# A pool mixer, SGU and PEER block: the last 32 gathers move from a stage of their own into the loop over the dense experts

## The chip, the cores and the metric

One NeuronCore of one Trainium2 chip runs the kernel. The metric is device time in microseconds, the median of several runs. Engines are named as in the profile: PE (TensorE matmuls), PEld (its weight loads), DVE (VectorE), ACT (ScalarE), POOL (GpSimd) and SP (SyncE, which only issues transfers here).

## The reference

1024 tokens of width 1024 pass a mixer (causal pooling over four windows beside a gated spatial unit) and then a PEER layer: 8 heads, each with two lists of 128 keys; the top 16 of each list are combined, the best 16 of the 256 pairs name 16 of 16384 experts, so a token uses 128 experts. An expert is one row of `peer_u` and one row of `peer_v`.

```python
q = (xb @ wq).reshape(T, PEER_HEADS, 2, D_HALF)
s = jnp.einsum('thpd,phkd->thpk', q, keys)
s_top, i_top = lax.top_k(s, PEER_TOPK)
...
idx = jnp.take_along_axis(cand_i, best_pos, axis=-1)
gate = jax.nn.softmax(best_s, axis=-1)
u = u_tab[idx]; v = v_tab[idx]
act = jax.nn.gelu(jnp.einsum('td,thkd->thk', xb, u))
return jnp.einsum('thk,thkd->td', (gate * act), v)
```

The layer's result is added to the residual and a last rmsnorm with `final_g` follows.

## The kernel before, in words

The 1024 tokens are eight blocks of 128. Two methods compute the PEER layer. Blocks 2 to 5 (512 tokens, "dense") run over all 16384 experts: `dense` (L604) goes through 128 groups `c` of 128 experts. For each it loads 512 KB of `uT` and 512 KB of `peer_v` (SP, three buffers `raw`), splits each into a high and a low part (ACT `uh`, `vh`, DVE `ul`, `vl`, L131 and L132), makes 24 matmuls into `mu` (`mm3`, L139 to L141), a GELU on ACT (L644), the product with the gates `gc` on DVE (L645) and a split into `wh`, `wl`. After every third `c` (`GROUP = 3`, L43) `down` makes 144 matmuls into `mm` and DVE adds them to `hD` (L623). 128 is not a multiple of 3, so the last two `c` have a `down` of their own. At the end four `finish` calls (L545: ACT square sum, a reciprocal root in twelve small DVE instructions, DVE scaling at L551, and a store by SP at L552) write blocks 2 to 5.

Blocks 0, 1, 6 and 7 ("sparse") fetch the chosen rows. `gather` (L475) is one indirect DMA issued by POOL that brings 128 rows of 4 KB into a buffer. A U part (`sparse_u`, L491) has 128 gathers of `peer_u`, one for each of a token's experts, and a DVE dot product after each (`junk`, L501). A V part (`sparse_v`, L513) has 128 gathers of `peer_v`, one for each token, taken four at a time (a quad): ACT writes the weights into `wz` (L520; two copies in turn), and PE adds the four tokens' sums into `po` (L531, 16 matmul records for a quad). When the 32 quads of a block are through, the residual is loaded, DVE adds `po` to it (L542) and `finish` follows. Only the four blocks' U and V parts gather: 1024 gathers in all.

`sparse(EARLY)` (L808) issues the first 320 of them ahead of the dense experts. `sparse(LATE)` (L814) is a generator with 704 steps, one gather each: the rest of U1, then V1 beside U6, V6 beside U7, and last V7 alone. The loop at L817 to L820 runs `dense`, and after each group `c` it advances the generator, so that `done * 128 <= (c + 1) * (704 - AFTER)`: 672 steps over 128 groups, 5.25 a group. The remaining `AFTER = 32` steps, all of V7, run in a stage of their own (L822 to L826) with a pool `gae` of 16 buffers `rowe`. That pool is opened on the right side after the pool `da` of `dense` has closed, so it lies where `da` lay, the tiles `hD` among it. Beside the dense experts the gathers use `rowv` (4 buffers) and `rowt` (7 buffers); V7 alone takes both in turn, quad by quad.

Nothing runs in the order in which it is written. The framework's scheduler orders the instructions of each engine by priority (program order) and by its own estimate of when each one could start, and each engine then runs its list in order. The matmuls of a quad carry a higher priority (L527), so they stand in PE's list where the scheduler thought their rows would have come.

Of the kernel before, what the change touches and what calls it, by code (L numbers as in the profile page):

```python
# [27 lines left out]
NK = 128  # L28
# [14 lines left out]
GROUP = 3  # L43
# [7 lines left out]

TURN = 6

ROWS, VROWS, EROWS = 7, 4, 16
QUAD = 4

EARLY = ({"U0": 128}, {"V0": 128, "U1": 64})
LATE = ({"U1": 64}, {"V1": 128, "U6": 128}, {"V6": 128, "U7": 128}, {"V7": 128})

AFTER = 32  # L60

RUNS = ((0, 1, 16), (1, 7, 8), (8, 8, 1))
NC = sum(na * nb for _, na, nb in RUNS)
# [3 lines left out]
def hybrid_block(ctx: ExitStack, tc: tile.TileContext, t: dict, out: bass.AP):  # L67
# [405 lines left out]
    homes = {"U": [(gat, "rowt", ROWS)], "V": [(gat, "rowt", ROWS)]}  # L473
# [189 lines left out]
    beside = []  # L663

    def sparse(phases):


        for phase in phases:
            n = max(phase.values())
            if beside:  # L670
                kinds = {name[0] for name in phase}
                homes["U"] = beside[:1] if len(kinds) > 1 else beside
                homes["V"] = beside[1:] if len(kinds) > 1 else beside
            for i in range(n):
                for name, m in phase.items():
                    unit = QUAD if name[0] == "V" else 1
                    for _ in range(((i + 1) * m // n // unit - i * m // n // unit) * unit):
                        if name not in parts:
                            parts[name] = [(sparse_u if name[0] == "U" else sparse_v)(int(name[1:])), 0]
                        part = parts[name]  # L680
                        next(part[0])
                        part[1] += 1
                        if part[1] == P:
                            for _ in part[0]:
                                pass
                        yield
# [93 lines left out]
    steps = 8 + P // TB  # L780
# [33 lines left out]
    gathered = sparse(LATE)  # L814
    steps = sum(sum(phase.values()) for phase in LATE)
    done = 0
    for c in dense(de, xdh, xdl):  # L817
        while done * NK < (c + 1) * (steps - AFTER):
            next(gathered, None)
            done += 1  # L820

    with tc.tile_pool(name="gae", bufs=EROWS, side="right", reuse_waits="tile") as gae:  # L822
        beside[:] = [(gae, "rowe", EROWS)]
        homes["U"] = homes["V"] = beside[:]
        for _ in gathered:
            pass  # L826
    gavs.close()
    des.close()

# [37 lines left out]
```

## Time and profile before

| | us |
|---|---|
| median of 3 runs (2700.18 to 2703.74) | 2702.26 |
| the profiled execution's own time | 2707.89 |
| its span | 2705.8 |
| POOL's last gather beside the dense experts starts | 2495.6 |
| the last matmul of the dense experts starts | 2635.6 |
| the first gather of the last stage starts | 2646.23 |

The span is the stretch of the trace, and the own time lies 2.09 us above it. The 40 slices of the profile's page are 67.6 us each; PE is busy in nine tenths or more of every slice from the seventeenth to the thirty-ninth, and three tenths of the last.

### The profile page before, as it was taken

The numbers are of one execution on the slowest core, as the hardware profiler recorded it, in microseconds if no ns is written. First come the engines' busy times: TensorE is split into PE (matmuls) and PEld (weight loads), VectorE is DVE, ScalarE is ACT, GpSimd is POOL, SyncE is SP. The second block draws the span as 40 slices with busy tenths as digits, with TensorE's granted clock in tenths as the row PEclk, the third lists the DMA queues.
The fourth block names the chain that finished last, engine by engine and source line by source line (L and its number), as shares of the span: only waits on it lengthen the run. The fifth ranks groups of instructions, "written<-read, shape, count | busy, mean of one in ns | idle before, by whom it ended". The sixth has DMA issues, their size and how long they took to land.

```text
span 2705.8 us, 34765 instructions
## 1 busy us (share of the span) xinstructions
PE 2438.1 (90%) x11968; PEld 1862.7 (69%) x11968; DVE 1896.4 (70%) x4643; ACT 774.3 (29%) x1424; POOL 1198.3 (44%) x1098
## 2 busy tenths in 40 slices
PE   7997899888866467999999999999999999999993
PEld 6886788767645144777777777777777777766770
DVE  2389979987797977986776767666676766433451
ACT  3220011245635252222222222322222222222220
POOL 0034753143443544655555555465455555344004
PEclk9998999999978689999999999999999999999996
DMA  7677998599988799999999999899999999889317
GB/s 250 210 245 230 384 344 284 168 313 315 333 286 296 255 307 348 361 356 324 365 354 342 341 339 364 328 361 375 327 342 359 349 348 331 324 329 359 119 39 287
DMA packets 345392, 831.49 MB, mean 307 GB/s; under 512 B 25216, under 2 KB 158848, under 8 KB 345216
## 3 DMA queue, kind: packets, MB, share of 16 engines
q0 software_dynamic: 147456, 536.94, 54.0%
q1 hardware_dynamic: 197760, 292.33, 31.4%
q8 instruction: 95, 1.56, 0.2%
q14 instruction: 81, 0.66, 0.1%
HBM read 785.13 MB, written 44.04 MB: 306 GB/s over the span
## 4 chain that ended last, share of the span: by engine, by line
PE 67%; DVE 15%; DMA 9%; issue 5%; ACT 2%; POOL 1%; SPq 0%; POOLq 0%; ACTq 0%; DVEq 0%
PE mm L176 8%; PE mm L139 8%; PE mm L140 8%; PE mu L141 8%; PE mm L141 8%; PE mu L139 8%; PE mu L140 8%; PE po L531 8%; DVE junk L501 3%; DMA G<-gs 2%; DMA rowt<-peer_v,idxT 2%; DVE rest L372 1%; PE mm L582 1%; DMA w<-w_out 1%; PE mu L582 1%
## 5 line engine op out<-in xcount | busy, mean ns | idle before, releaser
L480 POOL DMA_INDIRECT rowt<-peer_v,idxT x432 | 500.5, 1159 | 709.0 <-PE po L531 501.6
L480 POOL DMA_INDIRECT rowv<-peer_u,idx x288 | 353.6, 1228 | 176.4 <-DVE junk L501 105.7
L480 POOL DMA_INDIRECT rowt<-peer_u,idx x224 | 261.4, 1167 | 346.5 <-DVE top L370 166.4
L139 PE MATMUL mm<-vh,wh 128*128 128x512 f32 x1024 | 400.8, 395 | 14.4 <-ACT wh L131 8.4
L141 PE MATMUL mu<-xdh,ul 128*128 128x512 f32 x1024 | 403.0, 394 | 6.6 <-DVE ul L132 6.6
L139 PE MATMUL mu<-xdh,uh 128*128 128x512 f32 x1024 | 401.2, 393 | 6.2 <-ACT xdh L131 3.7
L140 PE MATMUL mu<-xdl,uh 128*128 128x512 f32 x1024 | 401.8, 392 | 1.2 <-DVE xdl L132 0.7
L140 PE MATMUL mm<-vl,wh 128*128 128x512 f32 x1024 | 401.0, 392 | 0.1
L501 DVE SCALAR_TENSOR_TENSOR junk<-rowv,h 128x1024 bf16<-128x1024 f32 x288 | 352.0, 1222 | 44.2 <-DMA rowv<-peer_u,idx 41.2
L141 PE MATMUL mm<-vh,wl 128*128 128x512 f32 x1024 | 376.9, 392 | 0.0
L623 DVE TENSOR_TENSOR hD<-hD,mm 128x512 f32<-128x512 f32 x344 | 225.8, 682 | 184.4 <-PE mm L141 183.5
L501 DVE SCALAR_TENSOR_TENSOR junk<-rowt,h 128x1024 bf16<-128x1024 f32 x224 | 271.9, 1214 | 19.6 <-DMA rowt<-peer_u,idx 18.2
L531 PE MATMUL po<-rowt,wz 128*32 128x512 f32 x1728 | 237.8, 650 | 38.0 <-DMA rowt<-peer_v,idxT 38.0
L139 PEld LDWEIGHTS mm<-vh,wh 128*128 128x128 f32 x1024 | 193.0, 189 | 75.1 <-issue 14.2
L141 PEld LDWEIGHTS mu<-xdh,ul 128*128 128x128 f32 x1024 | 192.6, 188 | 65.8 <-DVE ul L132 9.4
L139 PEld LDWEIGHTS mu<-xdh,uh 128*128 128x128 f32 x1024 | 192.1, 188 | 58.7 <-issue 9.2
L140 PEld LDWEIGHTS mu<-xdl,uh 128*128 128x128 f32 x1024 | 192.8, 188 | 53.8 <-issue 9.2
L141 PEld LDWEIGHTS mm<-vh,wl 128*128 128x128 f32 x1024 | 192.6, 189 | 50.1 <-issue 9.2
L140 PEld LDWEIGHTS mm<-vl,wh 128*128 128x128 f32 x1024 | 193.2, 189 | 42.4 <-issue 2.5
L644 ACT ACTIVATE a<-mu 128x512 f32<-128x512 f32 x128 | 76.0, 594 | 491.2 <-PE mu L141 490.0
L132 DVE SCALAR_TENSOR_TENSOR ul<-raw_u,uh 128x1024 fp32r<-128x1024 f32 x128 | 156.2, 1220 | 78.3 <-ACT uh L131 78.3
L131 ACT ACTIVATE vh<-raw_v 128x1024 fp32r<-128x1024 f32 x128 | 131.0, 1052 | 235.8 <-PE mm L141 216.9
(167 smaller groups left out, 3374.3 us busy)
## 6 DMA issues: line engine op xcount, KB each, us to landing
raw_u<-uT SPq DMA_DIRECT2D x128, 512.0 KB, 6.9
raw_v<-peer_v SPq DMA_DIRECT2D x128, 512.0 KB, 7.2
G<-gs SPq DMA_DIRECT2D x32, 1024.0 KB, 14.8
w<-wq SPq DMA_DIRECT2D x48, 512.0 KB, 6.6
w<-w_in SPq DMA_DIRECT2D x36, 512.0 KB, 4.8
w<-w_out SPq DMA_DIRECT2D x24, 512.0 KB, 6.6
h<-x SPq DMA_DIRECT2D x16, 512.0 KB, 7.7
rowt<-peer_v,idxT POOLq DMA_INDIRECT x432
```

Of the source, the lines that this page charges most:

```text
L131: nc.scalar.activation(hi, src, AF.Copy)
L132: nc.vector.scalar_tensor_tensor(lo, src, 1.0, f32(hi), op0=ALU.mult, op1=ALU.subtract)
L139: nc.tensor.matmul(dst, lh, rh, start=first and c == 0, stop=False)
L140: nc.tensor.matmul(dst, lh, rl, start=False, stop=False)
L141: nc.tensor.matmul(dst, ll, rh, start=False, stop=last and c == n - 1)
L176: mm = nc.tensor.matmul(dst[:, i, :], lhs, rhs, start=c == 0, stop=c == NDC - 1)
L480: ins = nc.gpsimd.indirect_dma_start(out=rowt, out_offset=None, in_=t[table], in_offset=bass.IndirectOffsetOnAxis(ap=ids, axis=0))
L501: nc.vector.scalar_tensor_tensor(junk, r, 1.0, h, op0=ALU.mult, op1=ALU.mult, accum_out=act[:, j:j + 1])
L531: mm = nc.tensor.matmul(po[g * 32:(g + 1) * 32, q * HALF:(q + 1) * HALF], z[:, g, 31 - j:63 - j], r[:, q * HALF:(q + 1) * HALF], start=j = ...
L582: mm = nc.tensor.matmul(p[:, i, :], oh[:, i, :], c, start=True, stop=True)
L623: nc.vector.tensor_add(hq, hq, p)
L644: nc.scalar.activation(a, p, AF.Gelu_apprx_tanh)
```

## The change

The stage at the end, its pool and the constants `AFTER` and `EROWS` go. All 704 steps of `sparse(LATE)` run in the loop over the dense experts, spread over the first 125 groups (`NK - GROUP`), so 5.632 a group. The last 32 gathers take `rowv` and `rowt` buffers like the other gathers of V7.

```diff
-ROWS, VROWS, EROWS = 7, 4, 16
+ROWS, VROWS = 7, 4
...
-
-AFTER = 32
...
     for c in dense(de, xdh, xdl):
-        while done * NK < (c + 1) * (steps - AFTER):
+        while done * (NK - GROUP) < min(c + 1, NK - GROUP) * steps:
             next(gathered, None)
             done += 1
-
-    with tc.tile_pool(name="gae", bufs=EROWS, side="right", reuse_waits="tile") as gae:
-        beside[:] = [(gae, "rowe", EROWS)]
-        homes["U"] = homes["V"] = beside[:]
-        for _ in gathered:
-            pass
     gavs.close()
     des.close()
```

## Rows read from the trace of the kernel before

**Rows 1.** Busy time by stretch: from:to, length, each engine's busy us (instructions), granted clock, DMA, GB/s
```profile
1200.00:2200.00 1000.00, 999.80 (x4789) 749.12 (x4791) 697.00 (x1007) 271.64 (x384) 546.11 (x457) 1.00 0.95 348
2300.00:2500.00 200.00, 200.00 (x1048) 141.08 (x1047) 84.66 (x115) 53.29 (x86) 89.06 (x87) 1.00 0.90 336
2500.00:2640.00 140.00, 135.72 (x613) 109.53 (x611) 68.89 (x115) 37.96 (x52) 0.00 (x0) 1.00 0.26 87
2640.00:2706.00 66.00, 23.38 (x128) 5.59 (x128) 8.69 (x35) 2.41 (x8) 29.96 (x32) 0.69 0.74 289
```

**Rows 2.** What PE waited for, 1200 to 2640 (all): us in total, times, longest
```profile
PE mm L139 <- ACT wh L131: 0.9, 1, 0.9
```

**Rows 3.** What POOL waited for, 2300 to 2706
```profile
POOL rowe L480 <- DMA out<-hD: 149.7, 1, 149.7
POOL rowv L480 <- PE po L531: 84.8, 13, 19.6
```

**Rows 4.** Timeline of the end: start us, us, engine, line, operation [idle before <- releaser]
```profile
2635.85 0.69 DVE L623 TENSOR_TENSOR hD<-hD,mm 128x512 f32<-128x512 f32 x1
...
2643.08 1.28 DVE L551 SCALAR_TENSOR_TENSOR hD<-hD,r,fgrow 128x1024 f32<-128x1024 f32 x1
2646.23 0.94 POOL L480 DMA_INDIRECT rowe<-peer_v,idxT  x1 [149.72 <-DMA out<-hD]
2647.47 0.94 POOL L480 DMA_INDIRECT rowe<-peer_v,idxT  x1 [0.30 <-issue]
...
2684.72 0.94 POOL L480 DMA_INDIRECT rowe<-peer_v,idxT  x1 [0.30 <-issue]
...
2692.78 3.40 PE L531 MATMUL po<-rowe,wz 128*32 128x512 f32 x16 [3.14 <-DMA rowe<-peer_v,idxT]
...
2696.28 1.22 DVE L542 TENSOR_TENSOR h<-h,po 128x1024 f32<-128x1024 f32 x1 [51.92 <-PE po L531]
...
2701.03 1.28 DVE L551 SCALAR_TENSOR_TENSOR h<-h,r,fgrow 128x1024 f32<-128x1024 f32 x1
```

**Rows 5.** PE's timeline around one pair of quads among dense matmuls
```profile
2488.11 0.39 PE L139 MATMUL mu<-xdh,uh 128*128 128x512 f32 x1
2488.43 1.94 PE L531 MATMUL po<-rowv,wz 128*32 128x512 f32 x16
2490.17 1.94 PE L531 MATMUL po<-rowt,wz 128*32 128x512 f32 x16
2492.04 0.50 PE L140 MATMUL mu<-xdl,uh 128*128 128x512 f32 x1
2492.38 0.40 PE L141 MATMUL mu<-xdh,ul 128*128 128x512 f32 x1
2492.62 0.40 PE L139 MATMUL mu<-xdh,uh 128*128 128x512 f32 x1
```

**Rows 6.** Gathers by buffer: ns min/median/max, first and last start; and rowv's quads on PE
```profile
L480 POOL DMA_INDIRECT rowe<-peer_v,idxT x32: 933/937/940, 2646.2 to 2684.7; - x32
L480 POOL DMA_INDIRECT rowv<-peer_v,idxT x48: 932/937/1984, 2296.5 to 2494.3; - x48
L531 PE MATMUL po<-rowv,wz x192: 592/592/618, 2319.9 to 2509.5; 128*32 128x512 f32 x192
```

**Rows 7.** The page's list of DMA queues: packets, MB, share of 16 engines
```profile
q0 software_dynamic: 147456, 536.94, 54.0%
```

**Rows 8.** Who waited in ACT and DVE, 1200 to 2500: us in total, times, longest
```profile
ACT wz L520 <- PE po L531: 183.4, 72, 9.9
DVE h L542 <- PE po L531: 7.2, 2, 6.3
```

**Rows 9.** Matmuls into mu, then into mm, 1200 to 2200: busy us (records)
```profile
1200.00:2200.00 1000.00, 463.60 (x1928) 1.00 0.95 348
1200.00:2200.00 1000.00, 464.29 (x1944) 1.00 0.95 348
```

**Rows 10.** Busy time early in the dense experts, and DVE's costliest groups there
```profile
1030.00:1180.00 150.00, 125.89 (x509) 98.16 (x509) 133.69 (x203) 40.01 (x51) 86.83 (x64) 0.95 0.96 353
...
L501 DVE SCALAR_TENSOR_TENSOR junk<-rowv,h 128x1024 bf16<-128x1024 f32 x33 | 40.2, 1219 | 0.3
L501 DVE DVE_READ_ACCUMULATOR junk<-rowv,h 128x1 f32 x32 | 2.6, 81 | 0.0
```

## The prediction

> **What bounds the kernel now.** I read the busy time by stretch first. From 1200 to 2200 us PE is busy 999.8 of 1000 us at a granted clock of 1.00 (2.4 GHz), while the DMA engines are at 0.95 and 348 GB/s [rows 1]. Both are nearly full, so the next question is which of them makes the other wait. The list of PE's waits answers it: from 1200 to 2640 PE waits once, for 0.9 us, and never for a row or a load [rows 2]. The dense experts are bound by PE's own list of matmuls.
>
> The end looks different. Between 2500 and 2640 POOL does nothing, the DMA engines fall to 0.26, and PE goes on; between 2640 and 2706 POOL and the DMA engines are back and PE has 23.4 of 66 us, at a mean granted clock of 0.69, so in part at 1.2 GHz [rows 1]. POOL's waits name the reason: one wait of 149.7 us, of the first gather into `rowe` for the store of `hD` [rows 3]. The pool `gae` lies where `hD` lay, so the last 32 gathers can't start before the dense result is on its way out, although POOL's last gather of the loop had started at 2495.6. The timeline of the end gives the order [rows 4]: the last scaling of `hD` ends at 2643.08 + 1.28 = 2644.36, the first late gather starts at 2646.23, the last quad at 2692.78, and block 7's own last scaling ends at 2702.31. The span ends at 2705.8. So some 61 us lie behind the dense result, and they are a chain of gathers, not matmul work.
>
> **The change part by part.** *What goes.* Everything between the end of the last scaling of `hD` (2644.36) and the same point of block 7 (2702.31), that is 57.95 us. Behind either there is one store, and 2705.8 - 2702.31 = 3.49 us until the span ends [rows 4]. I take 3.49 us behind `hD` too.
>
> *What is added to PE.* 32 gathers are 8 quads, 128 matmul records. PE is full, so they aren't hidden, and they push the dense end back. One pair of quads beside the dense experts shows the price [rows 5]: a dense matmul starts at 2488.11 and the next but for the pair at 2492.04, which is 3.93 us, where dense matmuls alone start 0.23 us apart (2492.38 to 2492.62 is 0.24, already nearly there). The pair costs 3.70 us plus 0.11 us for the slow step after it (2492.04 to 2492.38 is 0.34). A few hundredths more follow, so 3.9 us. Four pairs are 15.6 us. The bounds: 14.8 us (4 x 3.70) from below; from above, every quad alone with its own two switches, some 8 x (3.70/2 + 0.3) = 17.2 us. In the old stage the same quads ran at 0.69 of the clock and up to 3.40 us each [rows 4], which the change takes away without my counting it twice: it is in the 57.95.
>
> *What is added to POOL and the DMA engines.* V7's first 12 pairs have their `rowv` quads between 2319.9 and 2509.5 [rows 6], eleven steps of some 17 us. POOL waits 84.8 us in this part for PE to free a buffer [rows 3], so PE's list sets this pace, not the gathers. Four more pairs at 17 us put the last quad near 2511 + 4 x 17 = 2580, some 70 us ahead of a dense end near 2652. The bytes: 1024 gathers move 536.94 MB, 0.524 MB each [rows 7], so 32 are 16.8 MB. In 2500 to 2640 only 87 GB/s x 140 us = 12.2 MB move; with the gathers 29 MB in 156 us, 186 GB/s, where 336 and 348 run without a wait of PE [rows 1, 2]. I count POOL and transfers at nothing. Without that cover the price would be their own time at the old stage's rate, 16.8 MB / 289 GB/s = 58 us.
>
> The notes speak against such a cover. The Trainium skill, SBUF — State Buffer, section "SBUF: two separate sides", says that POOL writes the descriptors of its own DMAs and is locked out while certain VectorE operations run, so that such a gather stands still. The row bears it out in part: `rowv` gathers beside VectorE's work take 937 ns in the median like `rowe`, but up to 1984 against 940 [rows 6]. If all 32 were at that end, POOL would need 32 x 1.04 = 33 us more, and the last quad would come near 2613, still ahead of the dense end; by the median, nothing. This is why I give the rival of late quads some chance, and no more than that.
>
> *Waits that move along.* Eight `wz` copies on ACT each wait for the quad two before. Behind such a copy on ACT stand the splits and GELUs of the dense experts. ACT spent 183.4 us in 72 of these waits from 1200 to 2500 [rows 8], and PE lost 0.9 us by it [rows 2]. Eight more of them I count at nothing; the other end would be 8 waits of the mean 2.5 us on PE, 20 us, of which the rows show no trace. Block 7's close (a load of the residual and a store in SP's queue, 1.22 + 1.28 us and twelve small instructions on DVE, one square sum on ACT) now lies between dense work, and SP's store holds up the `raw` loads queued behind it. Blocks 1 and 6 close the same way inside the loop (the two waits of DVE for `po`, [rows 8]) without a wait of PE, so nothing again.
>
> *The new pace.* 704 steps over 125 groups are 5.632 gathers a group in program order instead of 5.25. I ask whether that pulls gathers ahead of dense work. From 1200 to 2200 PE made 1928 + 1944 matmuls, 48 a group, so 80.7 groups [rows 9], while POOL issued 457 gathers [rows 1]: 5.66 a group. The gathers already run at the new pace, ahead of the written order, so I count it at nothing too.
>
> **The sum.** 2644.36 + 15.6 + 3.49 = 2663.5 us of span; the own time is 2.09 us more, 2665.5. The median of the runs is 2702.26 against 2707.89 for the profiled execution, 5.6 us less, so 2659.9. I forecast 2660, 42 us or 1.6% faster. Own range 2653 to 2666: the bounds of the quads (-0.8, +1.6) and some 5 us for another order of the instructions.
>
> **The rivals.**
>
> *The early stretch gets worse.* From 1030 to 1180 DVE is busy 133.7 of 150 us and PE only 125.9 [rows 10]; U1's dot products take 1.219 + 0.081 = 1.30 us each there. If the new priorities put 0.38 more of them ahead of each group's splits, PE waits 0.5 us a group over some 12 groups: 6 us, 2666. For it: DVE is the bound there. Against: the DMA engines are at 0.96 already, so gathers can't come sooner. The same stretch could also gain, as PE idles 24 us in it: 2652 if a third of that goes.
>
> *The quads come late.* The scheduler might place the eight quads behind the last dense matmuls. Then 11 rows lie ready at 2636.5, the other 21 follow at 1.24 us each (the step from 2646.23 to 2647.47, [rows 4]) once the first quad is through (1.9): 2664.5. From the last gather's issue to its quad it was 2692.78 - 2684.72 = 8.1, and from there to the end 13.0: 2685.6 of span, 2682 as a median. For it: that list is an estimate made before the run. Against: in the loop the quads stand 17 us apart with 130 us of dense work left.
>
> *The memory is the bound.* If the transfers of the dense experts queue behind the added gathers, PE waits for `raw_u` and `raw_v`, the 58 us of transfers aren't hidden and the quads cost their 15.6 us on PE as well: 2644.4 + 58 + 15.6 + 3.5 = 2721.5 of span, 2718, slower than before. It decides for slower once more than 42 of the 58 us show as waits of PE. For it: 0.95 and 348 GB/s [rows 1]. Against: PE's single wait at that load [rows 2], and 0.26 where the gathers go. Beside it stands the Trainium skill, SBUF — State Buffer, section "A bandwidth-pool intuition that's wrong (but worth ruling out)": the memory off the chip is almost always the bottleneck from end to end. By that rule moving gathers would gain nothing; the trace doesn't agree for the stretch 2500 to 2640, where it moves 87 GB/s.
>
> **How the numbers follow.** The forecast has 0.70; the early stretch worse 0.10 (2666), or better 0.07 (2652); late quads 0.09 (2682); memory 0.04 (2718). The range 2652 to 2676 leaves out the late quads, the memory case and a little on either side of the rest, some 0.17. A measurement of this kernel can tell 0.2%, 5.4 us, from no change. Below 2696.9 lie all cases but the memory one, less a part of the late ones that comes out still later: faster 0.94, same 0.02, slower 0.04.
>
> **What would show it.** No tile `rowe`, and no wait of POOL for the store of `hD`. The quads of V7 go on at some 17 us a pair beyond 2511 and end near 2580. PE stays full until the dense end, near 2652, with 16 us more of work than before. Behind it come four closes, a store and the end. The prediction is wrong if PE waits for `raw` loads or rows after 2500, if block 7's close is again the last thing, or if the dense experts start or run slower ahead of 2500.

## The result and the profile after

The changed kernel takes 2660.7 us (median of 4 runs, 2649.12 to 2661.97) where the kernel before takes 2701.22 beside it: a ratio of 0.984, 95% interval 0.9811 to 0.987. That is 40.5 us less; 42 were forecast, and 2660. The profiled execution took 2661.97 us with a span of 2659.9. Two lines are gone from the code, so a line of before stands two numbers lower here (L531 is L529, L551 is L549).

Busy time by stretch of the changed kernel, in the columns of [rows 1]:

```profile
1200.00:2200.00 1000.00, 999.80 (x4792) 748.01 (x4791) 698.78 (x1008) 267.86 (x380) 544.32 (x456) 1.00 0.94 347
2300.00:2500.00 200.00, 198.61 (x1045) 139.41 (x1047) 79.27 (x97) 52.05 (x84) 89.58 (x88) 1.00 0.91 335
2500.00:2640.00 140.00, 140.00 (x692) 104.01 (x682) 63.47 (x88) 35.54 (x52) 28.49 (x29) 1.00 0.54 193
2640.00:2660.00 20.00, 7.70 (x33) 5.73 (x31) 14.48 (x60) 4.60 (x8) 0.00 (x0) 0.81 0.26 105
```

In the first line PE has 999.80 us as before, and the rest is close to it. In the third, POOL has gathers where it had none, the DMA engines are at 0.54 instead of 0.26, and PE is at 140.00 of 140 us, because the dense work now ends later. The stretch of gathers without dense work is gone.

What POOL waited for from 2300 on, and all that PE waited for from 1200 to 2655, in the columns of [rows 3] and [rows 2]:

```profile
POOL rowv L478 <- PE po L529: 118.0, 17, 18.2
```
```profile
PE mm L137 <- ACT wh L129: 0.9, 1, 0.9
PE po L529 <- DMA rowv<-peer_v,idxT: 0.8, 1, 0.8
PE po L529 <- DMA rowt<-peer_v,idxT: 0.6, 1, 0.6
```

The wait of 149.7 us for the store of `hD` has no successor; POOL's long waits are all for PE's quads. PE now waits twice for rows, 1.4 us together. Both waits fall on V7's eleventh pair of quads, at 2480 and 2483, ahead of the 8 added quads.

The timeline of the changed kernel's end, three parts, in the columns of [rows 4]: POOL's last gathers (three left out), the last two quads among dense matmuls on PE, and the last scaling of `hD`:

```profile
2556.70 0.98 POOL L478 DMA_INDIRECT rowv<-peer_v,idxT  x1 [10.44 <-PE po L529]
...
2562.15 0.93 POOL L478 DMA_INDIRECT rowt<-peer_v,idxT  x1 [0.30 <-issue]
```
```profile
2569.83 0.39 PE L138 MATMUL mu<-xdl,uh 128*128 128x512 f32 x1
2570.15 1.95 PE L529 MATMUL po<-rowv,wz 128*32 128x512 f32 x16
2572.02 0.50 PE L139 MATMUL mu<-xdh,ul 128*128 128x512 f32 x1
2572.36 0.39 PE L137 MATMUL mu<-xdh,uh 128*128 128x512 f32 x1
2572.59 0.40 PE L138 MATMUL mu<-xdl,uh 128*128 128x512 f32 x1
2572.92 1.94 PE L529 MATMUL po<-rowt,wz 128*32 128x512 f32 x16
```
```profile
2655.07 1.28 DVE L549 SCALAR_TENSOR_TENSOR hD<-hD,r,fgrow 128x1024 f32<-128x1024 f32 x1
```

The last gather starts at 2562, the last quad at 2572.92. Dense matmuls follow, the last of them at 2647.41, some 74 us later. The last scaling of `hD` ends at 2656.35, 3.55 us ahead of the end of the span.

One comparison holds for everything below. Each engine carries out a list that is fixed when the kernel is built. The first 10231 of PE's 11968 matmul records are the same before and after, in the same order; V7's first quad begins with record 10271 before and 10265 after. The lists of the other engines agree beyond 2300 us too. So whatever differs between the two executions ahead of that is no effect of the change. It isn't little: the first `rowv` quad of V7 starts at 2319.9 us before [rows 6] and at 2312.5 after. Most of it is there when the dense experts start, which the first addition to `hD` shows. A row has the shortest, median and longest time in ns, then the first and last start; the first start is 1060.6 before and 1054.0 after:

```profile
L623 DVE TENSOR_TENSOR hD<-hD,mm x344: 669/680/690, 1060.6 to 2635.9; 128x512 f32<-128x512 f32 x172
```
```profile
L621 DVE TENSOR_TENSOR hD<-hD,mm x344: 672/684/691, 1054.0 to 2647.8; 128x512 f32<-128x512 f32 x172
```

I therefore measure the end from V7's first quad to the start of the last scaling of `hD`, and let the runs judge the whole.

### The profile page after: what moved, and what is told of

Read it like the earlier page. It is cut to its first block, busy times and chain, and to the rows that moved or that the text cites. A ratio compares the mean times of both kernels' runs of the same rounds, so it can differ in the third digit from the quotient of the medians.

```text
span 2659.9 us, 34761 instructions
## 1 busy us (share of the span) xinstructions
PE 2427.4 (91%) x11968; PEld 1858.8 (70%) x11968; DVE 1897.3 (71%) x4643; ACT 773.7 (29%) x1424; POOL 1194.6 (45%) x1098
## 4 chain that ended last, share of the span: by engine, by line
PE 68%; DVE 15%; DMA 9%; issue 5%; ACT 2%; POOL 1%; SPq 0%; DVEq 0%; ACTq 0%; POOLq 0%
PE mm L137 8%; PE po L529 8%; PE mm L139 8%; PE mm L138 8%; PE mu L139 8%; PE mu L137 8%; PE mu L138 8%; PE mm L174 8%; DVE junk L499 3%; DMA rowt<-peer_v,idxT 2%; DMA G<-gs 2%; DMA w<-w_out 2%; DMA rowt<-peer_u,idx 1%; DVE rest L370 1%; PE mu L580 1%
## 5 line engine op out<-in xcount | busy, mean ns | idle before, releaser
L478 POOL DMA_INDIRECT rowt<-peer_v,idxT x448 | 512.4, 1144 | 714.2 <-PE po L529 502.4
L529 PE MATMUL po<-rowt,wz 128*32 128x512 f32 x1792 | 243.2, 643 | 35.6 <-DMA rowt<-peer_v,idxT 35.6
```

Source lines behind the costliest of these rows:

```text
L478: ins = nc.gpsimd.indirect_dma_start(out=rowt, out_offset=None, in_=t[table], in_offset=bass.IndirectOffsetOnAxis(ap=ids, axis=0))
L529: mm = nc.tensor.matmul(po[g * 32:(g + 1) * 32, q * HALF:(q + 1) * HALF], z[:, g, 31 - j:63 - j], r[:, q * HALF:(q + 1) * HALF], start=j = ...
```

## The experiments

**e0: the changed kernel again**, run beside the next three on the same chip.

> The changed kernel as it stands, run beside the others of this call so that they share a chip. Both theories: 2660 us, some 40 below the kernel before.

2662.67 us against 2705.32 before (0.9837, 0.9805 to 0.9868). Single runs of the unchanged before went from 2693 to 2719 there, so these medians are good to a few us.

**e1: only the pool goes.** Is it the wait, or the place in the code and the pace?

```diff
 # before.py
-    with tc.tile_pool(name="gae", bufs=EROWS, side="right", reuse_waits="tile") as gae:
-        beside[:] = [(gae, "rowe", EROWS)]
-        homes["U"] = homes["V"] = beside[:]
-        for _ in gathered:
-            pass
+    for _ in gathered:
+        pass
```

> The kernel before with its stage at the end left where it was written and with its old pace (672 gathers over 128 groups); only the stage's own pool goes, so its 32 gathers take rowv and rowt buffers. Theory 'memory': the whole loss was the wait for the memory of hD, and the place in the code and the pace are nothing, so 2660 us like the changed kernel (2653 to 2667). Rival 'place': gathers written behind the dense loop run behind it, and the new pace is what helped; then 2682 (the prediction's late quads) to 2701.

2663.49 us (0.9843, 0.9809 to 0.9878), beside 2662.67 for the changed kernel. The stage written behind the loop ran inside it. Its last gather is here, on POOL's timeline:

```profile
2561.92 0.94 POOL L480 DMA_INDIRECT rowt<-peer_v,idxT  x1 [0.30 <-PE mu L141]
```

2561.92, as in the changed kernel (2562.15). Theory "memory" stands: the overlap of `gae` with `hD` was the whole loss, as far as medians of six runs can tell. "Place" falls for these 32.

**e4: without the last quads and their gathers.**

```diff
 # after.py
-LATE = (..., {"V7": 128})
+LATE = (..., {"V7": 96})
...
-        for j in range(32):
+        n = 24 if b == 7 else 32
+        for j in range(n):
...
-                                              start=j == 0, stop=j == 31)
+                                              start=j == 0, stop=j == n - 1)
...
-                        if part[1] == P:
+                        if part[1] == (96 if name == "V7" else P):
```

> The changed kernel without the last 32 gathers of block 7 and without their 8 quads (block 7 lacks these 32 tokens' sums; its close stays). Theory 'PE pays': the quads are real work on a full PE, so it ends 15 to 20 us earlier than the changed kernel, 2640 to 2645 us. Rival 'hidden': PE's list has gaps that the quads fill, 2658 to 2660 us.

2645.5 us, 17.2 below e0: PE pays. In the trace the end is 323.4 us long, against 342.6 and 342.9 in the two profiles of the changed kernel. First the changed kernel, then e4: the quads by tile and the scalings of `hD`, each with ns min/median/max and its first and last start.

```profile
L529 PE MATMUL po<-rowv,wz x256: 590/592/618, 2312.5 to 2571.5; 128*32 128x512 f32 x128
```
```profile
L549 DVE SCALAR_TENSOR_TENSOR hD<-hD,r,fgrow x4: 1279/1280/1285, 2649.0 to 2655.1; 128x1024 f32<-128x1024 f32 x4
```
```profile
L530 PE MATMUL po<-rowv,wz x192: 592/592/618, 2314.3 to 2504.2; 128*32 128x512 f32 x192
```
```profile
L550 DVE SCALAR_TENSOR_TENSOR hD<-hD,r,fgrow x4: 1279/1282/1285, 2631.7 to 2637.7; 128x1024 f32<-128x1024 f32 x4
```

The stretch is the last start of the second line less the first start of the first: 2655.1 - 2312.5 and 2637.7 - 2314.3. The kernel before has 323.2 there, and PE's list of e4 is that of before, record for record, without the 128 records of the last stage. So e4's end is that of before with the late stage cut off.

**e5: the gathers without their quads.**

```diff
 # after.py, in sparse_v behind the four gathers
+            if b == 7 and j >= 24:
+                yield
+                continue
             with behind(f"V{b}", j) or tc.high_priority():
...
-                                              start=j == 0, stop=j == 31)
+                                              start=j == 0, stop=j == (23 if b == 7 else 31))
```

The `wz` copies of these quads on ACT stay.

> The changed kernel with the last 32 gathers issued and landed, but without the matmuls of their 8 quads (the sums of these tokens lack). Theory 'PE pays': POOL's work and the 16.8 MB are free beside the dense experts, so the time is that of the run without both, 2640 to 2645 us, within 4 us of it. Rival 'transfers': the gathers themselves hold up the dense loads, then 2655 to 2660 us.

2652.59 us, 7.1 above e4 and between the two forecasts. The six runs of e5 go from 2643 to 2661 us and those of e4 from 2638 to 2656, so the medians don't decide. The trace of e5, which is that of its fastest run, has 329.8 us for the end, 6.4 more than e4. Here are both, e5 first, from 2500 to 2550:

```profile
2500.00:2550.00 50.00, 47.93 (x205) 39.20 (x204) 27.98 (x44) 14.16 (x19) 25.09 (x26) 0.97 1.00 388
```
```profile
2500.00:2550.00 50.00, 50.00 (x237) 39.22 (x236) 27.52 (x44) 15.02 (x20) 0.00 (x0) 1.00 0.34 106
```

With no quads to wait for, little holds the gathers back: 26 of them keep POOL busy for 25 of 50 us, and the DMA engines are at 1.00 and 388 GB/s. PE loses 2.1 us there to a late `wh`. The chain that ends this wait holds no transfer: PE's last matmul into `mu`, then the GELU, the gate product and the split, and then the matmul that needs it.

```profile
2543.50 0.60 ACT L645 ACTIVATE a<-mu 128x512 f32<-128x512 f32 x1 [5.74 <-PE mu L139]
```
```profile
2544.13 0.69 DVE L646 TENSOR_TENSOR a<-a,gc 128x512 f32<-128x512 f32 x1 [4.51 <-ACT a L645]
```
```profile
2544.86 0.63 ACT L129 ACTIVATE wh<-a 128x512 fp32r<-128x512 f32 x1 [0.76 <-DVE a L646]
```
```profile
2543.08 0.39 PE L139 MATMUL mu<-xdh,ul 128*128 128x512 f32 x1
2545.54 0.55 PE L137 MATMUL mm<-vh,wh 128*128 128x512 f32 x1 [2.07 <-ACT wh L129]
2545.89 0.63 PE L138 MATMUL mm<-vl,wh 128*128 128x512 f32 x1
2546.31 0.63 PE L137 MATMUL mm<-vh,wh 128*128 128x512 f32 x1
...
2549.98 0.39 PE L137 MATMUL mu<-xdh,uh 128*128 128x512 f32 x1
```

The two stretches ahead of and behind that wait, in the columns of [rows 1]:

```profile
2540.00:2545.00 5.00, 3.46 (x16) 2.54 (x14) 0.69 (x1) 0.74 (x2) 2.81 (x3) 1.00 1.02 409
2546.00:2550.00 4.00, 4.00 (x13) 3.12 (x12) 3.71 (x4) 2.33 (x3) 0.00 (x0) 0.59 0.78 299
```

PE's list of e5 puts these `mm` straight behind the 24 matmuls into `mu` that they depend on. The wait costs more than its length: the twelve matmuls behind it take until 2549.98, 4.4 us instead of 12 x 0.23 = 2.8, and start up to 0.43 us apart. The granted clock is at 0.59 from 2546 to 2550, so mostly at 1.2 GHz, after 1.00 from 2540 to 2545. That is 1.7 us more. The rest of the 6.4 us is six matmuls more in the measured end (1.4), a wait of 0.9 for a row at 2476.8, ahead of these 32 gathers' quads, and one more split pair (some 0.3, worked out in the section on why the prediction was right). From 2500 to 2560 ACT, which makes the high parts, waits for no `raw` load. So in the trace the gathers by themselves make PE wait for no dense load, even at 388 GB/s, and the rival "transfers" isn't seen. What stays open is whether the scheduler's order of e5 comes from these gathers, and what e5's slower runs waited for. In the changed kernel the quads space the gathers out, at 344 GB/s from 2500 to 2550, and PE waits for nothing there.

**e6: 256 gathers written behind the loop.** How far does "the place is nothing" go?

```diff
 # e1
-AFTER = 32
+AFTER = 256
```

> As the run with the stage left in place and its pool gone, but 256 gathers instead of 32 are written behind the dense loop: all of V7, and the half of V6 and U7 that goes before it. Theory 'memory' with 'the place is nothing' at any number: 2660 us again. Rival 'the place counts once dot products stand behind the loop': the scheduler puts the 32 quads of V7 behind the last dense matmul; they cost 128 x 1.24 us = 159 us of gathers there, less the 32 quads' 62 us that PE saves beside the dense experts: 2660 + 97, so about 2757 us, slower than before.

2940.32 us (median of two runs; 1.087, 1.0833 to 1.0906): slower than before, and far more so than even the rival said. POOL's largest wait and two stretches:

```profile
POOL rowv L480 <- DVE rs_v L117: 387.8, 1, 387.8
```
```profile
2200.00:2400.00 200.00, 200.00 (x884) 165.61 (x883) 98.57 (x123) 58.35 (x74) 2.06 (x3) 1.00 0.39 126
...
2600.00:2700.00 100.00, 0.00 (x0) 0.00 (x0) 65.83 (x116) 0.00 (x0) 63.79 (x50) 0.50 0.82 273
```

The dot products of U7 have no higher priority, and those written behind the loop stand behind the dense work in DVE's list, up to its close. The gathers need their buffers, so POOL stands still for those 388 us, and U7's rest and all of V7 follow behind the dense work, PE's granted clock at 0.50 (1.2 GHz) from 2600 to 2700. The rival left the dot products out of its sum: U7's 64 late ones run from 2589 to 2716. It also priced V7's gathers at 1.24 us each; the 121 of them behind the dense work start from 2710 to 2923, some 1.8 us apart. The place counts, then, but for U parts, and for the V part that needs them. V6's late quads run inside the loop, by 2200, so a V part whose weights are ready is pulled forward, presumably by the priority of its matmuls (L527), which no run isolates.

**e7, e8, e9, e10: how many of U1's gathers go ahead of the dense experts.** With 80 us of the loop now free of gathers, the split of U1 (64 ahead, 64 in the loop) is open again.

```diff
 # after.py; n = 96, 128, 32, 0 (an entry of 0 is left out)
-EARLY = ({"U0": 128}, {"V0": 128, "U1": 64})
-LATE = ({"U1": 64}, ...
+EARLY = ({"U0": 128}, {"V0": 128, "U1": n})
+LATE = ({"U1": 128 - n}, ...
```

> The changed kernel with 96 instead of 64 of U1's gathers ahead of the dense experts (32 left for the loop). From 1000 to 1200 us PE idles some 28 us while VectorE is 87% busy with U1's dot products; the chain before that has VectorE 85% busy from 700 to 1000. Theory 'full PE': only PE's idle time can still be won, so 0 to 14 us less than the changed kernel, 2646 to 2660. Rival 'VectorE is the bound before the dense experts too': 32 x 1.3 = 42 us of dot products push their start back, by as much as VectorE has no room: 2660 to 2690.

> The same with all 128 of U1's gathers ahead of the dense experts. Theory 'full PE': 0 to 28 us less than the changed kernel, 2632 to 2660. Rival 'VectorE is the bound before them too': up to 83 us of dot products push the dense start back, 2660 to 2720.

> The changed kernel with 32 instead of 64 of U1's gathers ahead of the dense experts and 96 in the loop. The run with 96 ahead was slower, since VectorE is the bound ahead of the dense experts. Theory 'full PE': the end of the loop has some 80 us without gathers, so 32 more find room there, they cost PE nothing (dot products run on VectorE), and the dense experts start up to 32 x 1.3 = 42 us of VectorE earlier, less what PE then waits in a longer first stretch: 2640 to 2660 us. Rival 'VectorE is the bound in the first stretch as well': what is won ahead is lost there, 2660 to 2680.

> The same with none of U1's gathers ahead of the dense experts, all 128 in the loop. Theory 'full PE': 64 more gathers at 2.1 us are 134 us in the loop, more than the 80 us of room, so the last quads come behind the dense end or hold PE up: 2650 to 2690. Rival: VectorE's time ahead of the dense experts decides alone, 2620 to 2645.

More ahead is slower: 2678.79 us for 96 (0.9911, 0.9888 to 0.9935) and 2698.14 for 128 (0.9966). Fewer is faster: 2642.17 for 32 (0.9773, 0.9748 to 0.9798) and 2642.83 for 0 (0.9767, 0.9746 to 0.9789). The first addition to `hD` shows when the dense experts start; the rows are those of 128, then of none ahead:

```profile
L621 DVE TENSOR_TENSOR hD<-hD,mm x344: 671/681/690, 1110.9 to 2693.5; 128x512 f32<-128x512 f32 x172
```
```profile
L621 DVE TENSOR_TENSOR hD<-hD,mm x344: 673/684/692, 1010.3 to 2610.7; 128x512 f32<-128x512 f32 x172
```

1110.9, 1072.6, 1054.0, 1040.5 and 1010.3 us for 128, 96, 64, 32 and none, in one profile each: each 32 gathers of U push the start by 13 to 38 us, where six profiles with 64 lie between 1049 and 1061. DVE's busy time from 700 to 1000 us goes from 246 of 300 us for none and 243 for 32 to 267 for 128, so the rivals of e7 and e8 were right: DVE has little room there. e9 fits its first theory. None gains nothing over 32 in the runs: the dense work ends earlier, but the gathers last until 2608, PE waits 5.0 us for rows, and the last quad, at 2614.5, stands behind the last dense matmul. For e10 the time lies in the rival's range, yet the late quads are what the first theory forecast, with a loss well under what I had put on them. By the ratios to the kernel before, 0.977 against 0.984, both versions beat the changed kernel by some 0.7%, measured on another chip.

## Why the prediction was right

*What goes, 57.95 us.* Right, and the cause is shown: e1 takes away the pool alone and gains 41.8 us, as the changed kernel beside it gains 42.7. Behind the last scaling 3.55 us remain, 3.49 forecast.

*The quads on PE, 15.6 us.* The mechanism was right, the size too small: 17.2 us by the runs of e0 and e4, 19.4 by the traces. The pricing by pairs failed in two places. The pairs don't stay pairs: in V7, before, one of twelve is split by dense matmuls ([rows 5] show one that isn't); after, four of sixteen are, and each split costs PE some 0.3 us more. In the rows above 2569.83 to 2572.02 is 2.19 us for one quad, where half a pair is 3.93 / 2 = 1.97, and each half of a split pair has its own slow step of 0.34 us behind it (2572.02 to 2572.36), where 0.23 is usual. The second place is PE's waits for rows, 1.4 us. Of the 19.4, another 1.4 is no cost: PE's list has six more dense matmuls behind V7's first quad. Together, 15.6 + 3 x 0.33 + 1.4 + 1.4 gives the 19.4. From e4 to e1, which share that place, it is 16.7: one more split pair and one wait of 0.6.

*POOL and the transfers at nothing.* Right. From 2500 to the dense end PE's list of waits has no entry; the 1.4 us of waits for rows lie ahead of the added quads. That is the one trace of the prediction's last sign, dense experts that run slower ahead of 2500. The last quad came at 2573 where 2580 was forecast, and counted from V7's first quad both are 260 us. Gathers of `rowv` beside VectorE's work took 937 ns in the median and up to 1974. Of the 121 gathers from `peer_v` since 2290, the 23 over 1000 ns all ran beside a split, a gate product or a dot product of VectorE, which read two tiles from SBUF (48 gathers did so); none of the other 73 took over 947. The rule of the Trainium skill (SBUF — State Buffer, "SBUF: two separate sides") that VectorE can hold POOL's descriptors up may be at work in those few, though no run isolates it, and it decided nothing.

*Waits that move along.* Block 7's close and the eight `wz` copies now lie in the loop, and PE's list of waits has no entry for them.

*The new pace.* Nothing, as said, for a stronger reason than the one given: the order of PE's work is the same up to the start of V7. The 48 matmuls a group in that paragraph are 24 into `mu` and 24 into `mm`; a `down` therefore makes 72 after three groups, not the 144 named in the description of the kernel.

*The sum.* The profile came out at 2659.9 of span for 2663.5 forecast. That nearness is in part luck: the executions differ by several us ahead of V7 though their lists are equal (7.4 us less here), against 3.8 us too little for the quads. The median's nearness, 2660.7 for 2660, is luck once more: the profiled execution lies 1.3 us above its median, where 5.6 was taken from the kernel before.

*The rivals.* The early stretch has the same list. The last quad came 74 us ahead of the last dense matmul. The memory is no bound at 193 GB/s from 2500 to 2640, where PE is busy throughout. The trace doesn't agree here with the rule of the Trainium skill (SBUF — State Buffer, "A bandwidth-pool intuition that's wrong (but worth ruling out)") that the memory off the chip is almost always the bottleneck from end to end; even where e5 drives the DMA engines to 1.00, PE waits for no load.

## What to carry to other kernels

A buffer pool opened late can take the memory of something that ends late, and its first write then waits for that, however early the engine that writes is free; read the releaser of the first wait in a stage before the stage's work. Work that moves beside a full engine isn't free: price its instructions on that engine, singly and with the switches. A wait of PE can cost more than it lasts: in e5 one of 2.1 us was followed by matmuls at half the clock, 1.7 us more. And where a scheduler orders by readiness, the place in the code can mean nothing (e1, V7) or everything (e6, U7): compare the engines' orders, not the source.

## What was not expected of the hardware

Executions of one and the same list differ by up to 1%: before, 2693 to 2719 us over 11 runs on one chip. Six profiles have the same list of PE up to V7 (before, after, e0, e1, e4, e5). Their first addition to `hD` starts between 1049.0 and 1060.6 us, and from there to V7's first quad they take 1257.9 to 1259.8 us: the difference lies ahead of the dense experts. Indirect gathers and dense loads together drew 388 GB/s at a DMA share of 1.00 (e5, 2500 to 2550), above the 336 and 348 of the gather stretches in [rows 1].
